# 24 weight tiles of the middle part are split beside the first feed-forward, by way of DRAM and GpSimd's queue

## The chip, the cores and the metric

The kernel runs on one core of a Trainium2 chip. The metric is the device time of one execution in microseconds (us). The engines are named as in the profile: PE is TensorE, PEld its weight load, DVE is VectorE, ACT is ScalarE, POOL is GpSimd and SP is SyncE, which only issues transfers here. "Line 154" or L154 is a line of the kernel before.

## What is computed

One layer of a decoder trunk for 1024 prompt tokens and 8 sample tokens, with 1024 columns:

```python
h = layer_norm(ALPHA * x + 0.5 * swiglu(x, ffn1_wg, ffn1_wu, ffn1_wd), ln1_g, ln1_b)
q_a, k_a, v_a, q_i, k_i, w_i, q_r, k_r, v_r, g_r = jnp.split(h @ w_in, _split_points(), axis=-1)
o_a = attend(q_a, k_a, v_a, q_i, k_i, w_i)      # indexer scores pick 256 keys per query, then softmax
o_r, s_new = retention(qr, kr, vr, s0)          # 4 heads of 128, in chunks
y_r = jax.nn.silu(g_r) * (group_norm(o_r) * ret_gn_g)
mix = jnp.concatenate([o_a, y_r], axis=-1) @ w_out
h = layer_norm(ALPHA * h + mix, ln2_g, ln2_b)
h = layer_norm(ALPHA * h + 0.5 * swiglu(h, ffn2_wg, ffn2_wu, ffn2_wd), ln3_g, ln3_b)
```

Each feed-forward has 2816 hidden columns. All data are float32.

## The kernel before

**Numbers.** Each float32 operand of a product is taken apart: ScalarE casts it to a shorter format (the high part, `wh_...` for a weight), another engine subtracts the cast from the original (the low part, `wl_...`), and TensorE does three products, high by high, high by low and low by high (`mm3`, lines 169 to 171). This is called splitting here. A weight tile is 1024x128, 512 KB, held as 128 partitions by 1024 values in one slot of SBUF; a split tile is three slots: raw (`wr_...`), high, low.

**Tokens** are processed in three chunks of 344 columns (`CW`); a product of a weight tile with a chunk is 24 matmuls into one PSUM bank.

**Stages.** The first feed-forward runs chunk 0 alone (0 to 274 us) and then chunks 1 and 2 together (`chunks12`, 274 to 699 us). The second pass takes pairs of hidden tiles: for each of 11 pairs a chain of seven products for the gate (`chain(p, 'G')`), the down products of the pair before (`down_pair`), and a chain of seven for the other factor (`chain(p, 'U')`). Its weights come through a `Stream`, which fetches raw tiles on SP, splits them on ScalarE and VectorE (`whole` for a down tile, `seven` for the two raw tiles of a chain), and takes its slots from a free list `g.fs` (22 slots in this pass); `keep` is how many slots it leaves free when it works ahead. `keep` is 1 throughout, since `chunks12` is called with `tight=0`. After it come the first layer norm and the first head's tiles (699 to 787), the indexer's scores (787 to 890), heads 1 to 3 of the retention beside the top-k search (890 to 1147), the attention's tiles and the attention (1147 to 1345), the output projection (1345 to 1465 for its first eight tiles), and the second feed-forward (in all to 2310).

**The top-k search** (`topk`) is a loop over 32 bits: the keys below a threshold are counted, on ScalarE (line 1034) for the longer key blocks and on VectorE (line 1037) for the shorter, then two small instructions on VectorE (lines 1044 and 1045) move the threshold of every query.

**The tiles of the middle part.** From the scores to the output projection, weight tiles go through one object, `wq = Weights(g, tiles)`. `tiles` is the list in order of use: 3 indexer tiles (`qi1` to `qi3`), `gr0`, then key, value, query and gate of heads 1 to 3, 12 tiles of the attention (`va`, `qa`, `ka`), 8 of the output projection (`wo0` to `wo7`) and more. `fetch` issues the load of the next raw tile on SP into the one raw slot; `split` (through `w_split`) casts it on ScalarE (line 152) and subtracts on the engine of `g.lo_eng`, GpSimd in this stretch (line 154), into one of two pairs of slots, and fetches the next; `get` hands over the split pair. `tile(...)` gets the running tile, does its three chunks, and calls `split` for the next after the first of them.

**Order.** The program's text is run by a planner, `Sched`: each stage is a generator, a `yield` of a number of units (about a microsecond each) puts it off by that much, and `s.tick(cost)` behind each group of matmuls moves the planned time on and lets the generators that are due emit their instructions. `s.drain(e)` ticks until a generator is at its end. When the program is built, each engine's instructions are then put in an order of their own, so that an engine's order need not be that of the text.

The change touches `Weights`, `trunk` (the call of `chunks12`, the hook `ready`, which runs ahead of each chain step, and the list of tiles).

Of the kernel before, what the change touches and what calls it, by code (L numbers as in the profile page):

```python
# [15 lines left out]
F32 = mybir.dt.float32  # L16
F32R = mybir.dt.float32r
# [5 lines left out]
OP = mybir.AluOpType  # L23
# [3 lines left out]
P = 128  # L27
# [15 lines left out]
class Sched:  # L43


    def __init__(self):
        self.t = 0.0
        self.gens = []
# [32 lines left out]
def setbanks(g, **kinds):  # L81
    g.banks = kinds
    g.bi = {k: 0 for k in kinds}
# [14 lines left out]
def A(g, slot, name, dt=F32, n=NTOK):  # L98

    return g.ap.tile([P, n], dt, tag=f"a{slot}", name=name, bufs=1)  # L100


def A8(g, slot, name, dt=F32):
    return A(g, slot, name, dt, 1024).rearrange("p (k f) -> p k f", k=8)
# [7 lines left out]
def X8(g, slot, name, dt=F32):  # L112
    return X(g, slot, name, dt).rearrange("p (k t) -> p k t", k=8)
# [24 lines left out]
def w_raw(g, src, name):  # L138
    s = g.raws[g.ri % len(g.raws)]
    g.ri += 1  # L140
    raw = A8(g, s, f"wr_{name}")
    g.nc.sync.dma_start(raw if len(src.shape) == 3 else raw.rearrange("p (k h) f -> p k h f", k=src.shape[1]), src)
    return raw, name


def w_split(g, raw):

    raw, name = raw
    a, b = g.pairs[g.pi % len(g.pairs)]
    g.pi += 1  # L150
    hi = A8(g, a, f"wh_{name}", F32R)
    g.nc.scalar.copy(hi, raw)
    lo = A8(g, b, f"wl_{name}", F32R)
    g.lo_eng[g.pi % len(g.lo_eng)].tensor_tensor(out=lo, in0=raw, in1=hi.bitcast(F32), op=OP.subtract)  # L154
    return hi, lo
# [6 lines left out]
def wcols(w, col):  # L162
    return w[:, col:col + 128].rearrange("(k p) f -> p k f", p=P)
# [44 lines left out]
class Stream:  # L208
# [12 lines left out]
    def fetch(self):  # L221
        g = self.g
        while self.todo and self.held < self.nraw and len(g.fs) > self.keep:
            key, src = self.todo.pop(0)
            sl = g.fs.get()
            self.held += 1
            t = A(g, sl, f"wr_{key[0]}_{key[1]}", F32, 1024)
            g.nc.sync.dma_start(t.rearrange("p (k f) -> p k f", k=src.shape[1]), src)
            self.raw[key] = (t, sl)
# [311 lines left out]
def halves_of(t):  # L541
    return t[:, 0:4, :], t[:, 4:8, :]
# [189 lines left out]
def load_x(g, xp, xs, x, B, z):  # L732
# [10 lines left out]
    for b in range(3):  # L743
        fetch(b)
    yield 0.1
    for b in range(9):
# [22 lines left out]
        if b + 3 < 9:  # L769
            fetch(b + 3)  # L770
# [1129 lines left out]
    nc.sync.dma_start(ascr[:, :, 1024:1032].rearrange("h p b -> p h b"), on)  # L1900


class Weights:


    def __init__(self, g, tiles, split=True):
        self.g, self.tiles = g, tiles
        self.raw, self.ready = [], None
        self.fetch()
        if split:  # L1910
            self.split()

    def fetch(self):
        while self.tiles and len(self.raw) < len(self.g.raws):
            self.raw.append(w_raw(self.g, *self.tiles.pop(0)))

    def split(self):
        if self.raw:
            self.ready = w_split(self.g, self.raw.pop(0))
            self.fetch()  # L1920

    def get(self):
# [28 lines left out]
def trunk(tc, i, o):  # L1951
    nc = tc.nc
    g = G()
    g.nc, g.tc, g.s = nc, tc, Sched()
    s = g.s
    S_ = Scope(tc)
    w_in = i['w_in'][0]
    w_out = i['w_out'][0]
    cp = S_("cp")
    dp = S_("dp", space=bass.MemoryType.DRAM)  # L1960
# [33 lines left out]
    B = {'B22': halves_of(X8(g, "hh2", "opB22", F32R))}  # L1994
    B['B11'], B['B21'] = [tuple(t[:, 4 * q:4 * q + 4, :] for t in x[1]) for q in range(2)]
    f1 = Ffn2(g, i['ffn1_wg'][0], i['ffn1_wu'][0], i['ffn1_wd'][0], z, "f1")
# [44 lines left out]
    def ready(p, i):  # L2041
        need = {2: 'T2', 3: 'T1', 4: 'T3', 6: 'T4'}.get(i)
        s.until(lambda: need is None or need in B)

    f1.chunk0(x[0], hook, parked)
    psum['out'] = True
    setbanks(g, ch=[0, 1, 2, 3], dn=[4, 5], aux=[6, 7])
    f1.chunks12(B, ready)


    S_.close("msF")
# [23 lines left out]
    own = [q for q in g.fs.ids if q in ok][:6]  # L2075
# [95 lines left out]
                rX['qr0'] = w_raw(g, wcols(w_in, colX['qr0']), 'qr0')  # L2171


    tiles = [(wcols(w_in, 1536 + 128 * ct), f"qi{ct}") for ct in (1, 2, 3)] + [(wcols(w_in, 3656), "gr0")]
    for hd in (1, 2, 3):
        tiles += [(wcols(w_in, c0 + 128 * hd), f"{n}{hd}") for c0, n in ((2632, "kr"), (3144, "vr"), (2120, "qr"), (3656, "gr"))]
    for ct in range(4):
        tiles += [(wcols(w_in, c0 + 128 * ct), f"{n}{ct}") for c0, n in ((1024, "va"), (0, "qa"), (512, "ka"))]
    rows = [(w_out[128 * k:128 * k + 128, :].rearrange("p (k f) -> p k f", k=8), f"wr{k}") for k in (2, 3)]
    halves = [[(w_out[r:r + 512, 256 * j:256 * j + 256].rearrange("(k p) (h f) -> p k h f", p=P, h=2), f"wh{r}_{j}") for j in range(4)] for r in (0, 512)]  # L2180
    tiles += [(wcols(w_out, 128 * oo), f"wo{oo}") for oo in range(8)] + rows + halves[1]
    g.raws, g.ri, g.pairs, g.pi = [0], 0, PAIRS[:2], 0
    g.lo_eng = [nc.gpsimd]
    g.mixlo = [nc.vector]
    wq = Weights(g, tiles)

    def tile(evac, name, pace=0.0):
        w = wq.get()
# [27 lines left out]
    t = A(g, 6, "gT0")  # L2216
# [8 lines left out]
    hi, lo = {}, {}  # L2225
# [18 lines left out]
    for hd in (1, 2, 3):  # L2244
# [8 lines left out]
        t = A(g, 6, f"gT{hd}")  # L2253
# [42 lines left out]
    for ct in (1, 2, 3):  # L2296
# [4 lines left out]
        q = (qx[:, 0:1024], qx[:, 1024:2048]) if ct % 2 else (A(g, 9, f"q0{ct}", F32R, 1024), A(g, 1, f"q1{ct}", F32R, 1024))  # L2301
# [73 lines left out]
    for oo in range(6):  # L2375
        w = wq.get()
# [3 lines left out]
    w = [wq.get()]  # L2380
# [18 lines left out]
    w = [wq.get()]  # L2399
# [21 lines left out]
    for j in range(4):  # L2421
        w = wq.get()
# [7 lines left out]
    wq = Weights(g, halves[0], False)  # L2430
# [3 lines left out]
    B = {}  # L2434
# [43 lines left out]
    own = {}  # L2478
# [87 lines left out]
```

## Time and profile before

| | |
|---|---|
| median of 3 runs | 2312.18 us (2311.66 to 2313.08) |
| the profiled execution | 2311.91 us |
| its span | 2310.1 us |
| TensorE busy | 2220.8 us, 96% of the span |
| VectorE busy | 1761.8 us, 76% |
| ScalarE busy | 1072.4 us, 46% |
| GpSimd busy | 323.4 us, 14% |
| mean granted clock of TensorE | 0.985 |

The durations come from one profiled execution. The time of an execution is its span and some 1.8 us around it. A busy share is a mean over stages with different limits, so the stages have to be looked at one by one: which engine is full in it, and which wait ends last. A wait shown for an instruction is its engine's idle time just before it, with the instruction that released it.

### The profile page before, as it was taken

Reading aid. Unit: us, or ns where it says so; the run is one execution under the profiler, and the core shown is the slowest. Engines: PE = TensorE matmul, PEld = TensorE weight load, DVE = VectorE, ACT = ScalarE, POOL = GpSimd, SP = SyncE. Lnnn points to the kernel's source line nnn. Section 1 sums busy time; section 2 is a strip of 40 time slices with the busy share of each in tenths; the row PEclk is TensorE's granted clock in tenths of the full one; section 3 lists DMA queues with packets and bytes.
Section 4 is the critical chain, followed back from the end, with each engine's and each line's share of the span. In section 5 each row is a group of like instructions: output and inputs, shape, how many; then the busy total and the mean of one; then the engine's idle time right before and its main releaser. Section 6 shows DMA issues by size and latency. Waiting matters only on the chain.

```text
span 2310.1 us, 36886 instructions
## 1 busy us (share of the span) xinstructions
PE 2220.8 (96%) x14155; PEld 2144.3 (93%) x14155; DVE 1761.8 (76%) x3745; ACT 1072.4 (46%) x1931; POOL 323.4 (14%) x342
## 2 busy tenths in 40 slices
PE   8999999999999999889899999889999999999996
PEld 8999999999999989778789989879799999999996
DVE  5655797887878578678966678988568789887866
ACT  5433343332334465878466665343435444333331
POOL 0000100000002303444122234313210000000002
PEclk9999999999999999999999999989999999999998
DMA  8544332222222211121332142336544332222211
GB/s 266 156 136 146 109 89 74 83 75 64 82 75 97 93 25 46 53 69 49 88 89 56 51 141 80 121 123 189 177 129 137 98 103 80 92 73 65 92 65 49
DMA packets 239182, 224.32 MB, mean 97 GB/s; under 512 B 13098, under 2 KB 219774, under 8 KB 238238
## 3 DMA queue, kind: packets, MB, share of 16 engines
q1 hardware_dynamic: 235166, 209.38, 30.0%
q0 software_dynamic: 3840, 12.59, 1.7%
q8 instruction: 111, 1.82, 0.3%
q14 instruction: 65, 0.53, 0.1%
HBM read 200.91 MB, written 22.59 MB: 97 GB/s over the span
## 4 chain that ended last, share of the span: by engine, by line
PE 78%; DVE 11%; ACT 6%; issue 3%; DMA 1%; POOL 0%; POOLq 0%; SPq 0%; DVEq 0%; ACTq 0%
PE pds_f L403 5%; PE pds_f L404 5%; PE pds_f L405 5%; PE pg_f L169 2%; PE pu_f L169 2%; PE pg_f L170 2%; PE pg_f L171 2%; PE pdp_f L403 2%; PE pu_f L171 2%; PE pu_f L170 2%; PE pdp_f L404 2%; PE pdp_f L405 2%; ACT ja L1034 2%; PE ps_f1U L169 2%; PE ps_f2G L170 2%
## 5 line engine op out<-in xcount | busy, mean ns | idle before, releaser
L407 DVE SCALAR_TENSOR_TENSOR z<-pds_f,z 128x344 f32<-128x344 f32 x320 | 164.6, 516 | 125.9 <-PE pds_f L405 124.7
L403 PE MATMUL pds_f<-gs_f,wh_f1ds 128*128 128x344 f32 x352 | 114.1, 325 | 0.1
L407 DVE SCALAR_TENSOR_TENSOR z<-pdp_f,z 128x344 f32<-128x344 f32 x160 | 80.0, 512 | 44.1 <-PE pdp_f L405 43.9
L403 PE MATMUL pds_f<-gs_f,wh_f2ds 128*128 128x344 f32 x352 | 113.4, 322 | 0.0
L405 PE MATMUL pds_f<-gs_f,wl_f1ds 128*128 128x344 f32 x352 | 113.2, 322 | 0.0
L404 PE MATMUL pds_f<-gs_f,wh_f1ds 128*128 128x344 f32 x352 | 113.1, 321 | 0.0
L405 PE MATMUL pds_f<-gs_f,wl_f2ds 128*128 128x344 f32 x352 | 112.4, 319 | 0.0
L404 PE MATMUL pds_f<-gs_f,wh_f2ds 128*128 128x344 f32 x352 | 112.4, 319 | 0.0
L1034 ACT ACTIVATE ja<-key,zt 128x1024 bf16<-128x1024 int16 (+5 forms) x90 | 93.7, 1041 | 34.6 <-DVE zt L1045 33.1
L723 POOL TENSOR_TENSOR yt<-yt,ln_b_rows 128x512 f32<-128x512 f32 (+1 forms) x9 | 12.0, 1352 | 570.3 <-ACT yt L722 570.3
L296 ACT CAST wS_f1G<-ws_f1G 128x512 fp32r<-128x512 f32 x44 | 25.0, 618 | 133.5 <-PE pds_f L404 68.1
L1508 ACT CAST p<-pT 128x512 fp32r<-128x512 f32 (+2 forms) x112 | 47.4, 433 | 54.1 <-PE pT L1504 41.9
L296 ACT CAST wS_f2G<-ws_f2G 128x512 fp32r<-128x512 f32 x44 | 25.7, 619 | 93.4 <-PE pds_f L405 80.7
L403 PEld LDWEIGHTS pds_f<-gs_f,wh_f1ds 128*128 128x128 f32 x352 | 66.8, 190 | 1.1 <-DVE z L407 0.3
L404 PEld LDWEIGHTS pds_f<-gs_f,wh_f1ds 128*128 128x128 f32 x352 | 66.7, 190 | 0.2
L405 PEld LDWEIGHTS pds_f<-gs_f,wl_f1ds 128*128 128x128 f32 x352 | 66.7, 189 | 0.0
L403 PEld LDWEIGHTS pds_f<-gs_f,wh_f2ds 128*128 128x128 f32 x352 | 66.2, 188 | 0.2 <-ACT gs_f L465 0.2
L404 PEld LDWEIGHTS pds_f<-gs_f,wh_f2ds 128*128 128x128 f32 x352 | 66.2, 188 | 0.0
L405 PEld LDWEIGHTS pds_f<-gs_f,wl_f2ds 128*128 128x128 f32 x352 | 66.1, 188 | 0.0
L612 POOL TENSOR_TENSOR lns_l<-z 128x344 f32<-128x344 f32 x3 | 2.8, 929 | 442.2 <-DVE z L407 428.0
L1509 DVE TENSOR_TENSOR p<-pT,p 128x512 fp32r<-128x512 f32 (+2 forms) x112 | 54.5, 497 | 8.7 <-ACT p L1508 7.5
L1470 ACT ACTIVATE z<-z,mn 128x896 f32<-128x896 f32 (+3 forms) x64 | 49.8, 778 | 20.0 <-DVE mn L1467 15.7
(815 smaller groups left out, 8651.0 us busy)
## 6 DMA issues: line engine op xcount, KB each, us to landing
wr_f1g<-in_ffn_wg_dram SPq DMA_DIRECT2D x22, 512.0 KB
wr_f1u<-in_ffn_wu_dram SPq DMA_DIRECT2D x22, 512.0 KB
wr_f1dp<-in_ffn_wd_dram SPq DMA_DIRECT2D x22, 512.0 KB
wr_f1G<-in_ffn_wg_dram SPq DMA_DIRECT2D x22, 512.0 KB
wr_f1U<-in_ffn_wu_dram SPq DMA_DIRECT2D x22, 512.0 KB
wr_f1ds<-in_ffn_wd_dram SPq DMA_DIRECT2D x22, 512.0 KB
wr_f2u<-in_ffn_wu_dram SPq DMA_DIRECT2D x22, 512.0 KB
wr_f2g<-in_ffn_wg_dram SPq DMA_DIRECT2D x22, 512.0 KB
```

The source lines that it names most:

```text
L169: g.nc.tensor.matmul(ps, w[0][:, k, :], x[0][:, k, :], start=first and i == 0, stop=False)
L170: g.nc.tensor.matmul(ps, w[0][:, k, :], x[1][:, k, :], start=False, stop=False)
L171: g.nc.tensor.matmul(ps, w[1][:, k, :], x[0][:, k, :], start=False, stop=last and i == n - 1)
L296: nc.scalar.copy(t[:, 0], src)
L403: g.nc.tensor.matmul(ps, wh[:, o, :], th, start=i == 0, stop=False)
L404: g.nc.tensor.matmul(ps, wh[:, o, :], tl, start=False, stop=False)
L405: g.nc.tensor.matmul(ps, wl[:, o, :], th, start=False, stop=i == len(grp) - 1)
L407: g.nc.vector.scalar_tensor_tensor(out=z, in0=ps, scalar=0.5 / ALPHA, in1=z, op0=OP.mult, op1=OP.add)
L1034: nc.scalar.activation(jk[:, 0:n], key[b], AF.Sign, bias=t[:, j:j + 1], scale=-1.0, accum_out=cnt[:, j:j + 1])
L1470: nc.scalar.activation(z[:, 0:n], z[:, 0:n], AF.Exp, bias=prev, scale=-1.0, accum_out=mn[:, 3:4])
L1508: nc.scalar.copy(ph[:, js, ts], ptv[:, js, ts])
L1509: nc.vector.tensor_tensor(out=pl[:, js, ts], in0=ptv[:, js, ts], in1=ph[:, js, ts].bitcast(F32), op=OP.subtract)
```

## The change

A generator `presplit` is started ahead of the first feed-forward. From the second pair of the two-chunk pass on (`g.plain` is false for p >= 1), once five slots of `g.fs` are free, it takes three of them. For each of 24 tiles (all of `tiles` but the attention's 12 and those after `wo7`) it fetches the raw tile with a transfer issued by GpSimd, casts it on ScalarE, subtracts on VectorE, fetches the next raw tile, and stores the high and the low part to a scratch in DRAM (`wscr`), again with transfers issued by GpSimd. The pauses are 2.0 and 13.5 units a tile. `chunks12` is called with `tight=11`, so that `keep` is 4 instead of 1 in all the gate chains, and `s.drain(ahead)` behind the pass lets the generator finish.

`Weights` is told in `made` which tiles lie split in the scratch. Such a tile is loaded as two parts of 512 KB by two transfers on SP, straight into its pair of slots, where a raw tile was cast and subtracted before; `fetch` leaves it alone. The order in which tiles are used is the same. The other 12 tiles of the attention, and those after `wo7`, are done as before.

```diff
+def presplit(g, tiles, wscr, made):
+    nc = g.nc
+    while g.plain or len(g.fs) < 5:
+        yield 0.5
+    own = [g.fs.get() for _ in range(3)]
+    def fetch(n):
+        raw = A8(g, own[0], f"pr_{tiles[n][1]}")
+        nc.gpsimd.dma_start(raw, tiles[n][0])
+        return raw
+    raw = fetch(0)
+    yield 8.0
+    for n, (src, name) in enumerate(tiles):
+        hi, lo = A8(g, own[1], f"ph_{name}", F32R), A8(g, own[2], f"pl_{name}", F32R)
+        nc.scalar.copy(hi, raw)
+        nc.vector.tensor_tensor(out=lo, in0=raw, in1=hi.bitcast(F32), op=OP.subtract)
+        yield 2.0
+        if n + 1 < len(tiles):
+            raw = fetch(n + 1)
+        for j, t in enumerate((hi, lo)):
+            nc.gpsimd.dma_start(wscr[n, j], t.rearrange("p k f -> p (k f)").bitcast(F32))
+        made[name] = (wscr[n, 0], wscr[n, 1])
+        yield 13.5
+    g.fs.put(*own)
 class Weights:
     def fetch(self):
-        while self.tiles and len(self.raw) < len(self.g.raws):
+        while self.tiles and self.tiles[0][1] not in self.made and len(self.raw) < len(self.g.raws):
             self.raw.append(w_raw(self.g, *self.tiles.pop(0)))
     def split(self):
-        if self.raw:
-            self.ready = w_split(self.g, self.raw.pop(0))
+        g = self.g
+        if not self.raw and self.tiles and self.tiles[0][1] in self.made:
+            name = self.tiles.pop(0)[1]
+            pair = g.pairs[g.pi % len(g.pairs)]
+            g.pi += 1
+            self.ready = tuple(A8(g, q, f"w{j}_{name}", F32R) for j, q in enumerate(pair))
+            for t, src in zip(self.ready, self.made[name]):
+                g.nc.sync.dma_start(t.rearrange("p k f -> p (k f)").bitcast(F32), src)
+            self.fetch()
+        elif self.raw:
+            self.ready = w_split(g, self.raw.pop(0))
             self.fetch()
     def ready(p, i):
         need = {2: 'T2', 3: 'T1', 4: 'T3', 6: 'T4'}.get(i)
         s.until(lambda: need is None or need in B)
+        g.plain = p < 1
+    made = {}
+    g.plain = True
+    ahead = s.add(presplit(g, list(tiles), dp.tile([len(tiles), 2, P, 1024], F32, name="wscr"), made))
-    f1.chunks12(B, ready)
+    f1.chunks12(B, ready, 11)
+    s.drain(ahead)
-    wq = Weights(g, tiles)
+    wq = Weights(g, tiles, True, made)
```

The list of the 24 tiles now stands ahead of the first feed-forward, and the attention's 12 tiles are put back into their place in it when `wq` is made.

## Rows read from the trace of the kernel before

**Rows 1.** The page, part 1: busy time, share and instructions by engine.

```profile
PE 2220.8 (96%) x14155; PEld 2144.3 (93%) x14155; DVE 1761.8 (76%) x3745; ACT 1072.4 (46%) x1931; POOL 323.4 (14%) x342
```

**Rows 2.** Busy us (instructions) by stage: PE, PEld, DVE, ACT, POOL; clock, DMA, GB/s.

```profile
0.00:274.00 274.00, 266.53 (x1678) 263.31 (x1679) 165.49 (x230) 113.99 (x168) 7.48 (x12) 0.99 0.55 165
...
274.00:699.00 425.00, 424.74 (x2696) 424.04 (x2695) 349.40 (x638) 157.99 (x277) 1.25 (x1) 1.00 0.27 79
...
787.00:890.00 103.00, 99.42 (x603) 93.03 (x602) 72.19 (x155) 60.38 (x113) 18.59 (x13) 0.98 0.13 35
...
890.00:1147.00 257.00, 228.43 (x1536) 212.02 (x1534) 210.06 (x555) 178.77 (x357) 103.40 (x115) 0.95 0.23 63
...
1345.00:1465.00 120.00, 110.61 (x755) 103.96 (x754) 100.19 (x371) 68.33 (x150) 42.28 (x48) 0.99 0.37 114
```

**Rows 3.** The chain of waits from 890 to 1147, its shares by line.

```profile
by line: ACT ja L1034 20.1%; issue 11.4%; DVE jv L1037 3.3%; DVE tief L1070 3.0%; DVE zt L1045 2.6%; DVE key L1054 2.2%; DVE zt L1044 2.0%; DVE tie L1069 2.0%; DVE tie L1068 1.7%; DVE tie L1075 1.7%; DVE o L1203 1.7%; DVE zt L982 1.5%; DVE 
```

**Rows 4.** Instructions of lines 154, 152: duration ns min/median/max, first and last start.

```profile
L154 POOL TENSOR_TENSOR wl_kr<-wr_kr,wh_kr x3: 2367/2382/2398, 873.8 to 1022.2; 128x1024 fp32r<-128x1024 f32 x3
...
L152 ACT CAST wh_kr<-wr_kr x4: 1045/1048/1051, 699.2 to 1020.2; 128x1024 fp32r<-128x1024 f32 x4
```

**Rows 5.** Timelines of DVE and POOL (start, us, engine, line), and line 1044's durations.

```profile
943.29 2.30 DVE L1044 TENSOR_TENSOR zt<-zt 128x6 f32<-128x6 f32 x1 [1.48 <-ACT ja L1034]
...
943.20 2.37 POOL L154 TENSOR_TENSOR wl_kr<-wr_kr,wh_kr 128x1024 fp32r<-128x1024 f32 x1
...
L1044 DVE TENSOR_TENSOR zt<-zt x32: 119/166/2359, 920.5 to 1107.1; 128x6 f32<-128x6 f32 x32
...
1065.79 2.40 DVE L627 SCALAR_TENSOR_TENSOR zt<-zt 128x8 f32<-128x8 f32 x1
```

**Rows 6.** Pieces of the chain of waits (start, us, what); TensorE's timeline.

```profile
929.53 0.95 ACT wh_gr L152
...
941.28 1.04 ACT wh_kr L152
...
1062.97 0.95 ACT wh_qr L152
...
961.29 0.40 PE L169 MATMUL pw_kr<-h1h,wh_kr 128*128 128x344 f32 x1
```

**Rows 7.** VectorE's timeline near 894 and 1416, and durations of lines 982 and 1680.

```profile
894.28 2.01 DVE L982 SCALAR_TENSOR_TENSOR zt<-rl,wsgn,zt 128x320 f32<-128x320 f32 x1 [1.94 <-ACT rl L977]
...
L982 DVE SCALAR_TENSOR_TENSOR zt<-rl,wsgn,zt x70: 543/677/2677, 807.5 to 899.0; 128x512 f32<-128x512 f32 x21, 128x384 f32<-128x384 f32 x21, 128x448 f32<-128x448 f32 x14, 128x320 f32<-128x320 f32 x14
...
1416.48 2.25 DVE L1680 SCALAR_TENSOR_TENSOR zt<-zt 128x1 f32<-128x1 f32 x1
...
L1680 DVE SCALAR_TENSOR_TENSOR zt<-zt x16: 146/160/2887, 1407.6 to 1492.9; 128x1 f32<-128x1 f32 x16
```

**Rows 8.** SP's timeline, busy time (as rows 2), and the gathers of tile s3kv.

```profile
913.52 0.37 SPq L142 DMA_DIRECT2D wr_gr<-in_w_in_dram  x1
...
914.50:917.00 2.50, 1.20 (x7) 1.21 (x8) 2.50 (x5) 0.00 (x0) 1.25 (x2) 1.00 0.79 210
...
L1788 POOL DMA_INDIRECT s3kv<-in_cache_k_dram,zt x16: 940/984/1869, 1541.5 to 1581.9; - x16
...
DMA to landing us min/median/max: 3.6/4.0/4.3
```

**Rows 9.** VectorE's groups from 312 to 690 (count | busy us, mean ns).

```profile
L274 DVE TENSOR_TENSOR wl_f1ds<-wr_f1ds,wh_f1ds 128x1024 fp32r<-128x1024 f32 x20 | 24.4, 1222 | 3.0 <-ACT wh_f1ds L273 2.9
```

**Rows 10.** Busy time in two stretches of the feed-forwards (as rows 2).

```profile
300.00:313.00 13.00, 13.00 (x85) 13.00 (x84) 12.74 (x26) 7.31 (x15) 0.00 (x0) 1.00 0.27 82
...
1844.00:1975.00 131.00, 131.00 (x841) 130.80 (x840) 115.95 (x229) 57.66 (x95) 0.00 (x0) 1.00 0.31 96
```

**Rows 11.** Timelines of ScalarE and TensorE at the end of the two-chunk pass.

```profile
688.18 1.06 ACT L152 CAST wh_ki<-wr_ki 128x1024 fp32r<-128x1024 f32 x1
...
698.83 0.32 PE L171 MATMUL ps_f1U<-opT,wA_f1U 128*128 128x344 f32 x1
```

More of the change, by code (lines that the diff above doesn't have):

```diff
@@ L1900, in s3_attend, with __init__ @@
     nc.sync.dma_start(ascr[:, :, 1024:1032].rearrange("h p b -> p h b"), on)
+def presplit(g, tiles, wscr, made):
[21 more added lines that the diff above has]
+    g.fs.put(*own)
 class Weights:
-    def __init__(self, g, tiles, split=True):
-        self.g, self.tiles = g, tiles
+    def __init__(self, g, tiles, split=True, made={}):
+        self.g, self.tiles, self.made = g, tiles, made
         self.raw, self.ready = [], None
@@ L2043, in ready @@
         s.until(lambda: need is None or need in B)
+        g.plain = p < 1
+    tiles = [(wcols(w_in, 1536 + 128 * ct), f"qi{ct}") for ct in (1, 2, 3)] + [(wcols(w_in, 3656), "gr0")]
+    for hd in (1, 2, 3):
+        tiles += [(wcols(w_in, c0 + 128 * hd), f"{n}{hd}") for c0, n in ((2632, "kr"), (3144, "vr"), (2120, "qr"), (3656, "gr"))]
+    tiles += [(wcols(w_out, 128 * oo), f"wo{oo}") for oo in range(8)]
+    made = {}
+    g.plain = True
+    ahead = s.add(presplit(g, list(tiles), dp.tile([len(tiles), 2, P, 1024], F32, name="wscr"), made))
     f1.chunk0(x[0], hook, parked)
@@ L2171, in trunk @@
                 rX['qr0'] = w_raw(g, wcols(w_in, colX['qr0']), 'qr0')
[L2174 to L2178, printed above, removed]
     rows = [(w_out[128 * k:128 * k + 128, :].rearrange("p (k f) -> p k f", k=8), f"wr{k}") for k in (2, 3)]
     halves = [[(w_out[r:r + 512, 256 * j:256 * j + 256].rearrange("(k p) (h f) -> p k h f", p=P, h=2), f"wh{r}_{j}") for j in range(4)] for r in (0, 512)]
-    tiles += [(wcols(w_out, 128 * oo), f"wo{oo}") for oo in range(8)] + rows + halves[1]
+    tiles = tiles[:16] + [t for ct in range(4) for t in ((wcols(w_in, 1024 + 128 * ct), f"va{ct}"), (wcols(w_in, 128 * ct), f"qa{ct}"), (wcols(w_in, 512 + 128 * ct), f"ka{ct}"))] + tiles[16:] + rows + halves[1]
     g.raws, g.ri, g.pairs, g.pi = [0], 0, PAIRS[:2], 0
```

## The prediction

> **What bounds the kernel now.** I read the page first: TensorE is busy for 96% of the span and GpSimd for 14% [rows 1], so the question is only where TensorE is not busy. The busy time by stage answers that [rows 2]. In the first feed-forward's two-chunk pass (274 to 699 us) TensorE has no gap: 2696 matmuls in 425 us, 6.34 per us, with VectorE at 349 of 425 us. In the score stage (787 to 890) it lacks 3.6 of 103 us, in the stage with heads 1 to 3 beside the top-k search (890 to 1147) 28.6 of 257 at a mean granted clock of 0.95, and beside the output projection (1345 to 1465) 9.4 of 120. The 24 tiles of the change are used in these last three stages. In the top-k stage the chain of waits does not run mainly through matmuls: the counts on ScalarE hold 20.1% of it, more than any other line [rows 3]. The loop is serial: ScalarE counts keys against a threshold, VectorE compares the counts and moves the threshold, then come the next counts. What stands in that loop lengthens the stage.
>
> **What is removed.** Each of the 24 tiles now costs a cast on ScalarE (1.05 us) and a subtraction on GpSimd (2.38 us) [rows 4], 25 us and 57 us in all. Neither engine is full there, so the sum is not these totals but what of them stands on the chain.
>
> First the subtractions. While GpSimd subtracts, VectorE can stand still: its threshold instruction on 128x6 values normally takes 0.166 us (the median) and took 2.30 us at 943.29, from 0.09 us after the start of a 2.37 us subtraction to its end [rows 5]. It happens four times in this stage to instructions of about 0.17 us, first here and last at 1065.79 (2.40 us) [rows 5]. All four fall on subtractions of this change's tiles and lie on or beside the chain; without these the instructions would give back 2.13 us (the first) to 2.23 (the last), 8.7 us together.
>
> Then the casts. Four of them are pieces of the chain in this stage, between two counts or ahead of the threshold, the first at 929.53, the last at 1062.97, 0.95 to 1.05 us each: 4.0 us [rows 6]. Together 12.7 us in the serial loop.
>
> Outside this loop three more VectorE instructions are held by subtractions: two score accumulations (2.01 us at 894.28, where 0.54 is the shortest, and the longest of them, 2.68 us where 0.68 is the median) and a 128x1 step of the sample's search at 1416.48 (2.25 us, median 0.16) [rows 7]: 1.5 + 2.0 + 2.1 = 5.6 us. I take nothing of it: in the score stage TensorE lacks only 3.6 of 103 us, so the matmuls take over the chain at once, and at the output projection the attention's own work runs beside the search. The bounds are therefore 4.0 (the casts alone: GpSimd's other work, 103 us busy in this stage less 12 subtractions of 2.4, moves up and holds VectorE instead) and 12.7 + 5.6 = 18.3 us. I take 12.7, since in the loop nothing else runs in parallel and TensorE has 28.6 us of gaps there to give.
>
> **What is added where the tiles are used.** Each tile is now two loads of 512 KB on SP in place of one. A 512 KB load issued at 913.52 moved data from 914.5 to 917 [rows 8], so about 3.4 us; a pair about 6 us. It can start when TensorE is done with the tile two before, as the cast can; the tile cast at 941.28 has its first matmul at 961.29 [rows 6], 20 us later. So the running tile's matmuls hide the loads and I cost them at nothing. Without that cover it would be some 6 us for each tile that finds SP late, for SP is in order and stores that wait for VectorE stand in front of the loads. The 12 tiles that stay (values, queries, keys of the attention) keep cast and subtraction.
>
> **What is added in the pass.** 24 casts (25 us of ScalarE) and 24 subtractions on VectorE at 1.22 us (29 us), 24 fetches and 48 stores issued by GpSimd, 38 MB. GpSimd has no work of its own there (1.25 us of 425), so nothing is moved behind these issues. The pass already does 20 whole-tile splits of exactly this shape between 312 and 690, with 1.22 us on VectorE each [rows 9], without a gap on TensorE. VectorE goes from 349 to 378 of 425 us, 89%. The second feed-forward ran like this: with six slots taken (eighteen left; nineteen here) and the same reserve of four, VectorE stood at 116 of 131 us, and TensorE did 841 matmuls in it, 6.42 per us, no slower [rows 10]. The traffic would be 79 + 89 = 168 GB/s, and the first pass of this feed-forward runs at 165 GB/s with TensorE busy. So the longer reserve and the three slots cost nothing by these rows. What can hurt is a subtraction in a stretch in which VectorE is full, as it is in the first chains of a pair (12.74 of 13 us [rows 10]). About a third of the 24 fall there, 8 x 1.22 = 9.8 us at most; four PSUM banks cover most of it. Between 0 and 9.8 I take 2, near the row of the second feed-forward.
>
> The change adds one wait that matters: ScalarE's cast waits for a fetch that GpSimd issued. Behind it in ScalarE's queue are the gate's silu and the casts of the products, behind these VectorE's products, and behind those TensorE's PSUM banks. No plain transfer issued by GpSimd is in this trace. The nearest are its gathers of 256 KB: 0.94 to 1.87 us to issue and 3.6 to 4.3 us to land [rows 8]. The fetch has 1024 pieces of 512 bytes where a gather has 128, so an issue may well be longer. After the cast there is a second wait of the same kind, for the store of the tile before.
>
> One rule of the Trainium skill speaks against the change. The trace first: beside a VectorE that is busy most of the time, the slowest gather took 1.87 us to issue and the quickest 0.94 [rows 8], so something can hold an issue for 0.9 us. "SBUF — State Buffer", section "SBUF: two separate sides", says that a transfer issued by GpSimd can stand until VectorE ends an instruction that uses both its ports, and the section "Summary: rules for kernel authors" says to issue from SP or ScalarE instead. The section "Who interferes with whom" does not count a subtraction of two tensors among these instructions, and two-tensor work is all that VectorE does in the pass, so by this page's own terms the rule would hardly bite here; no run shows it yet. If it bites, it is rival 5.
>
> **Sum.** The profiled execution took 2311.91 us (span 2310.1), 0.27 below the median of 2312.18. Against it: -12.7 + 2 = -10.7, so 2301.2; set against the median 2301.5 us.
>
> **The rivals.**
> 1. Late fetches: slower. The program's text is not the order on the engines: a cast whose line stands after the pass runs at 688.18, ten us before the pass's last matmuls end [rows 11]. So each engine's instructions were put in order beforehand, by when they were thought ready, and the splits will be pulled forward as far as their three slots allow. If a fetch then lands later than thought, ScalarE stands with the pass's work behind it. Each fetch waits for the subtraction before it, so lateness adds up: from 12.7 / 24 = 0.53 us a tile on, all is lost. With 0.6 us (a gather's 4.0 us landing against 3.4 from SP) plus 0.9 us (its slowest issue over its fastest), 1.5 x 24 = 36 us: 2312 - 12.7 + 36 = 2335.5. For it: an unseen kind of issue. Against it: nothing in the pass waits for a transfer now. Chance 0.18.
> 2. Another engine's work takes the place: GpSimd's rotations, decays and gathers move up and hold VectorE as the subtractions did, or TensorE's order in the stage binds; 4.0 us gained, 2 lost: 2310. Chance 0.17.
> 3. Everything on the chain is won: -18.3 and no loss in the pass: 2294. Chance 0.13.
> 4. Engine order follows the text at the pass's end. The splits are paced at 15.5 units, but a wait ends only at the next tick (1.89 in a chain, 0.94 in a down pass), so some 18; the pass has 426 units, the splits start near 40 (26.5 for the first pair, then seven steps, when by my count of the stream's slots five are first free) and only 21 of 24 fit. Three would then stand between the pass and its last part, two of them behind a fetch: 2.3 + 2 x (1 + 4.0 + 2.3) = 16.9 us less two PSUM groups of 1.9: +13, so 2312 + 13 + 2 - 12.7 = 2314. The row at 688.18 speaks against it. Chance 0.05.
> 5. Each issue in the pass is held as the slowest gather was, by 0.93 us, and all three of a tile stand in the loop of fetch, split and store: 24 x 3 x 0.93 = 67 us, so 2312 - 12.7 + 67 = 2366. That is the Trainium skill's rule of above. Against it: the pass has no VectorE instruction of one input alone. Chance 0.04.
>
> **How the numbers follow.** The forecast, 2301.5, has 0.43. A measurement of this kernel can tell about 0.2% (4.6 us) from no change. Faster: forecast and rival 3, 0.56. Same: rivals 2 and 4, 0.22. Slower: rivals 1 and 5, 0.22. The range goes from a little more than the whole chain won (2291) to a lateness of about 1 us a tile (2324).
>
> **What would show it.** Right: no subtraction of these tiles on GpSimd after 787, no threshold instruction of 2.3 us beside them, the stage from the first sort key to the last mask shorter by about 11 us, and 6.3 matmuls per us in the pass. Rival 1: the pass longer than 425 us and ScalarE's casts of the new tiles waiting for transfers. Rival 2: 2.3 us threshold instructions beside other GpSimd work. Rival 4: a hole of TensorE at the end of the pass. The prediction is wrong if the pass loses more than the top-k stage gains, which hangs on one number that the trace before does not hold: how long a 512 KB fetch issued by GpSimd takes.

## The result, and the profile after

The changed kernel is slower: median 2341.07 us (2338.76 to 2345.27) beside 2312.3 us for the kernel before on the same chip, ratio 1.0124, 95% interval 1.0112 to 1.0136. The profiled execution is the longest of the four, 2345.27 us with a span of 2343.4, 33.4 more than the span before. The prediction had the sign wrong, and its range (2291 to 2324) did not reach the time.

| profiled execution, us from its start | before | after | later by |
|---|---|---|---|
| last chain matmul of the two-chunk pass ends | 699.15 | 745.72 | 46.6 |
| first matmul of `ki` | 729.89 | 779.24 | 49.4 |
| first sort key | 885.48 | 929.40 | 43.9 |
| last mask of the search | 1156.59 | 1166.19 | 9.6 |
| first matmul of tile `va0` | 1108.18 | 1133.20 | 25.0 |
| first matmul of `wo0` | 1364.87 | 1397.52 | 32.7 |
| end | 2310.06 | 2343.42 | 33.4 |

The busy times of the whole execution hardly tell the two kernels apart; the page's first part answers to [rows 1]:

```profile
PE 2230.4 (95%) x14155; PEld 2152.1 (92%) x14155; DVE 1759.7 (75%) x3769; ACT 1072.4 (46%) x1931; POOL 315.2 (13%) x390
```

The table of times does: by the first matmul of `ki` the pass has lost 49 us, the stages up to the first matmul of `va0` win 24, and 8 of these are given back up to the first matmul of `wo0`. First the loss: the stage from 274 to 699 again (columns as in [rows 2]), then a stretch with down products and the stretch with chains behind it.

```profile
274.00:699.00 425.00, 391.94 (x2400) 385.89 (x2399) 331.25 (x594) 160.29 (x269) 49.04 (x73) 0.98 0.51 159
357.00:383.00 26.00, 23.32 (x147) 22.73 (x146) 15.32 (x28) 6.61 (x11) 5.94 (x9) 1.00 0.64 197
383.00:407.00 24.00, 23.39 (x148) 22.97 (x146) 24.00 (x46) 13.38 (x24) 0.00 (x0) 1.00 0.43 138
...
435.00:455.00 20.00, 16.85 (x107) 16.51 (x106) 20.00 (x38) 10.19 (x19) 0.00 (x0) 1.00 0.37 118
```

TensorE does 2400 matmuls in the 425 us in which it did 2696. There are two kinds of stretch: from 357 to 383 VectorE is busy for only 15.3 of 26 us, and from 383 to 407 and 435 to 455 it is full. What it did not do in the first it has to do in the second, and there TensorE waits for it (busy for 16.9 us from 435 to 455). The whole pass up to its last chain matmul, after and before:

```profile
274.00:745.70 471.70, 438.64 (x2696) 432.59 (x2695) 368.10 (x660) 180.53 (x302) 49.04 (x73) 0.98 0.49 151
```

```profile
274.00:699.10 425.10, 424.83 (x2696) 424.14 (x2695) 349.50 (x638) 157.99 (x277) 1.25 (x1) 1.00 0.27 79
```

Of the 46.6 us, 32.8 are idle time of TensorE. For the other 13.8 it is busy longer with as many matmuls, at a mean granted clock of 0.98 in place of 1.00; how much of this the clock alone takes is not separated here.

What it waits for stands in the timeline of one such stretch: ScalarE, GpSimd, VectorE and TensorE of the changed kernel. L1912 is the fetch of `presplit`, L1919 its cast, L1920 its subtraction, L1925 its stores; in brackets the idle time ahead and what ended it.

```profile
364.11 1.05 ACT L1919 CAST ph_kr<-pr_kr 128x1024 fp32r<-128x1024 f32 x1 [3.45 <-DMA pr_kr<-in_w_in_dram]
372.28 1.05 ACT L1919 CAST ph_vr<-pr_vr 128x1024 fp32r<-128x1024 f32 x1 [7.12 <-DMA pr_vr<-in_w_in_dram]
380.37 1.05 ACT L1919 CAST ph_qr<-pr_qr 128x1024 fp32r<-128x1024 f32 x1 [7.04 <-DVE z L407]
```

```profile
365.45 0.53 POOL L1925 DMA_DIRECT2D wscr<-ph_kr  x1 [5.14 <-ACT ph_kr L1919]
366.93 0.91 POOL L1912 DMA_DIRECT2D pr_vr<-in_w_in_dram  x1 [0.95 <-DVE pl_kr L1920]
367.83 0.54 POOL L1925 DMA_DIRECT2D wscr<-pl_kr  x1
```

```profile
365.41 1.23 DVE L1920 TENSOR_TENSOR pl_kr<-pr_kr,ph_kr 128x1024 fp32r<-128x1024 f32 x1 [1.68 <-DMA wscr<-pl_gr]
...
373.58 1.23 DVE L1920 TENSOR_TENSOR pl_vr<-pr_vr,ph_vr 128x1024 fp32r<-128x1024 f32 x1 [1.85 <-DMA wscr<-pl_kr]
```

```profile
367.11 0.43 PE L403 MATMUL pds_f<-gs_f,wh_f1ds 128*128 128x344 f32 x1 [1.26 <-DVE z L407]
375.29 0.42 PE L403 MATMUL pds_f<-gs_f,wh_f1ds 128*128 128x344 f32 x1 [1.43 <-DVE z L407]
```

The splits do not stand 15.5 units apart, as the text paces them. In the engines' own order they are packed three or four to a stretch of down products: of the 23 steps from one cast to the next, 16 are under 12 us, with a median of 8.19. One turn reads: subtraction done at 366.6, fetch issued at 366.93, low part's store issued right behind it at 367.83, cast at 372.28, when the fetch is in. The cast ends at 373.33, and the subtraction waits until 373.58 for the store of the low part of the tile before. Behind it in VectorE's order stand the accumulations of the down products (line 407), behind these TensorE. All over the pass:

```profile
ACT ph_wo L1919 <- DMA pr_wo<-in_w_out_dram: 54.2, 8, 9.7
ACT ph_gr L1919 <- DMA pr_gr<-in_w_in_dram: 20.0, 4, 8.4
ACT ph_vr L1919 <- DMA pr_vr<-in_w_in_dram: 19.3, 3, 8.9
```

```profile
PE pds_f L403 <- DVE z L407: 17.3, 12, 2.4
PE ps_f1G L169 <- DVE pc_f1U L469: 14.8, 6, 4.0
```

These are views of the waits, ScalarE's (three of its rows) and TensorE's: waiting instruction, releaser, us in total, times, longest. ScalarE stands 132 us in all, in 22 waits, ahead of the new casts for fetches, TensorE 17.3 us for accumulations in the down products and 14.8 us for VectorE at the chains' start.

The gain is of the kind that was forecast. Lines 1044 and 1045 in the changed kernel, and the search from its first sort key to its last mask, before and after:

```profile
L1044 DVE TENSOR_TENSOR zt<-zt x32: 152/166/783, 960.0 to 1120.4; 128x6 f32<-128x6 f32 x32
L1045 DVE SCALAR_TENSOR_TENSOR zt<-zt x32: 157/166/875, 960.2 to 1120.8; 128x6 f32<-128x6 f32 x32
```

```profile
885.50:1156.60 271.10, 241.54 (x1624) 223.76 (x1622) 223.98 (x589) 185.47 (x378) 103.40 (x115) 0.96 0.23 63
```

```profile
929.40:1166.20 236.80, 214.14 (x1478) 202.48 (x1477) 197.10 (x549) 166.72 (x338) 76.44 (x103) 0.96 0.27 85
```

No threshold instruction takes 2.3 us any more (783 and 875 ns at most, where [rows 5] show 2359), and the search is 34 us shorter. Not all of the 34 us is won: the search now holds 146 matmuls fewer, and the stretch from its last mask to the first matmul of `wo0` holds 145 more, before and after:

```profile
1156.59:1364.87 208.28, 202.53 (x1380) 189.45 (x1378) 140.52 (x431) 131.28 (x310) 55.88 (x72) 1.00 0.28 81
```

```profile
1166.19:1397.52 231.33, 225.63 (x1525) 209.77 (x1523) 152.00 (x471) 139.15 (x337) 56.06 (x72) 0.99 0.30 88
```

TensorE is busy for 97% of this stretch in both kernels, so the matmuls that left the search lengthen it: by 23 us. The pairs of loads that took the casts' place are issued early enough, as this line of SP's timeline shows (two loads, 0.80 us together). The first matmul of `kr1` comes at 938.99, and none of TensorE's waits from 730 to 1600 us ended with a transfer:

```profile
916.88 0.80 SPq L1953 DMA_DIRECT2D w_kr<-wscr  x2
```

### The profile page after: what moved, and what is told of

Its sections match the earlier page's. It is cut to its first block, busy times and chain, and to the rows that moved or that the text cites. A ratio compares the mean times of both kernels' runs of the same rounds, so it can differ in the third digit from the quotient of the medians.

```text
span 2343.4 us, 37108 instructions
## 1 busy us (share of the span) xinstructions
PE 2230.4 (95%) x14155; PEld 2152.1 (92%) x14155; DVE 1759.7 (75%) x3769; ACT 1072.4 (46%) x1931; POOL 315.2 (13%) x390
## 4 chain that ended last, share of the span: by engine, by line
PE 53%; DVE 12%; ACT 7%; DMA 5%; issue 3%; POOL 1%; POOLq 0%; DVEq 0%; ACTq 0%; SPq 0%
PE pds_f L403 3%; ACT ja L1034 3%; PE pds_f L404 3%; PE pds_f L405 3%; PE ps_f2U L170 2%; PE ps_f2G L170 2%; PE ps_f2G L169 2%; PE ps_f2U L171 2%; PE ps_f2G L171 2%; PE ps_f2U L169 2%; PE pg_f L169 1%; PE pg_f L170 1%; PE pu_f L169 1%; PE pg_f L171 1%; PE pdp_f L403 1%
## 5 line engine op out<-in xcount | busy, mean ns | idle before, releaser
L169 PE MATMUL pg_f<-xh,wh_f1g 128*128 128x344 f32 x176 | 57.0, 324 | 2.1 <-ACT xh L762 2.1
L169 PE MATMUL pg_f<-h2h,wh_f2g 128*128 128x344 f32 x176 | 58.5, 332 | 0.0
```

Source lines behind the costliest of these rows:

```text
L169: g.nc.tensor.matmul(ps, w[0][:, k, :], x[0][:, k, :], start=first and i == 0, stop=False)
```

## The experiments

Theory L, formed after the result: a split's cast and subtraction wait for transfers that arrive late, and the pass's own work stands behind them. The rivals are the plain work of the splits, the slots they take, and the stores. All times are medians; the kernel before was measured beside each group, and its median lies between 2312.3 and 2314.8 us.

**The cost alone.** The tiles are split and stored, and done again later as before.

```diff
-    wq = Weights(g, tiles, True, made)
+    wq = Weights(g, tiles, True, {})
```

> The splits in the first feed-forward are made and stored, but nothing uses them: all 24 tiles are cast and subtracted later as in the kernel before. So this is the price of the pass by itself. Theory L (late transfers: ScalarE and VectorE stand at a split until its fetch and the store of the tile before have landed, with the pass's own work queued behind them): the pass ends some 47 us later, as it does in the changed kernel (745.7 for 699.2), and nothing gives it back: 2312 + 47 = 2359, between 2352 and 2366. The forecast's price of the pass was 2 us: 2314.

Measured: 2367.04 beside 2314.77 us (1.0229, 1.0212 to 1.0246). The last chain matmul ends at 748.51. The kernel loses 52 us, 1 more than the end of L's range and 50 more than forecast.

**The gain alone.** In `presplit`, only the first tile:

```diff
     for n, (src, name) in enumerate(tiles):
+        if n:
+            made[name] = (wscr[0, 0], wscr[0, 1])
+            continue
...
-        if n + 1 < len(tiles):
-            raw = fetch(n + 1)
```

> Only the first tile is split and stored in the feed-forward; all 24 are then loaded from its place in the scratch, so 23 of the tiles hold wrong weights. This is the gain of the use by itself. In the changed kernel the delay falls from 49 us ahead of the scores to 33 at the output projection, so theory L expects 16 us of gain: 2296, between 2293 and 2300. The forecast's 12.7 us would give 2299.5. If what was gained beside the top-k search is given back later whatever stands ahead, 2305 to 2312.

Measured: 2296.85 us (0.9929, 0.9912 to 0.9945), 17.9 less than before. Cost and gain nearly add up: 52.3 - 17.9 = 34.4, for 28.8 between the medians and 33.4 between the spans of the changed kernel. Loading each tile as a pair costs nothing that shows. This kernel keeps the larger reserve, and takes the three slots for its one tile: its first matmul of `ki` comes at 734.74, 4.9 us later than before, and from there to the end it wins 20.1 us. The 17.9 are thus a gain of 20 less a small part of the price.

**The slots alone.** The body of `presplit` between taking and giving back the slots becomes 24 pauses.

```diff
+    for _ in tiles:
+        yield 15.5
```

> The three slots are taken for as long as in the changed kernel and the longer reserve stays, but nothing is fetched, split, stored or used. Theory L: no price, 2312, between 2309 and 2315. Rival R (the three slots and the reserve of four starve the pass's own stream of weights): most of the 47 us, 2340 or more.

Measured: 2317.85 us (1.0014, 1.0004 to 1.0023), 3.1 more than before. That is above L's range and far below R's: taking three slots and a longer reserve is not quite free, but it is no cause of 50 us.

**The work alone**: one fetch, one pair of stores, 24 casts and subtractions.

```diff
-        if n + 1 < len(tiles):
-            raw = fetch(n + 1)
         for j, t in enumerate((hi, lo)):
-            nc.gpsimd.dma_start(wscr[n, j], ...)
-        made[name] = (wscr[n, 0], wscr[n, 1])
+            if n == 0:
+                nc.gpsimd.dma_start(wscr[n, j], ...)
+        made[name] = (wscr[0, 0], wscr[0, 1])
```

> One tile is fetched once and stored once, but all 24 casts and 24 subtractions are made, from that one raw tile, and all 24 tiles are loaded later from the one place in the scratch, so 23 tiles hold wrong weights. It has the work of the splits on ScalarE and VectorE without any wait for a transfer. Theory L: the work alone costs 0 to 6 us, so with 16 us of gain 2296 to 2302. Rival W (54 us more work on two engines that were already the second bound, above all 29 us on VectorE): 20 us or more of the 47, so 2316 or more.

Measured: 2300.06 us (0.9939, 0.9923 to 0.9956), 3.2 above the gain alone. The pass, by its busy times and by the first casts on ScalarE's timeline:

```profile
274.00:700.00 426.00, 424.31 (x2687) 422.83 (x2686) 369.98 (x659) 180.68 (x301) 3.46 (x4) 1.00 0.26 82
```

```profile
323.19 1.05 ACT L1919 CAST ph_gr<-pr_qi 128x1024 fp32r<-128x1024 f32 x1 [1.29 <-DVE pl_qi L1920]
325.53 1.05 ACT L1919 CAST ph_kr<-pr_qi 128x1024 fp32r<-128x1024 f32 x1 [1.29 <-DVE pl_gr L1920]
327.87 1.05 ACT L1919 CAST ph_vr<-pr_qi 128x1024 fp32r<-128x1024 f32 x1 [0.94 <-DVE pl_kr L1920]
```

The splits are packed closer still, 2.34 us apart, and TensorE is busy for 424.3 of 426 us all the same. So neither the work nor its packing by itself is the cause: rival W falls, and the 41 us up to 2341 come with the transfers (43.5 if each kernel is counted from the kernel before of its group).

**Fetch or store.** First the edit without refetching (the two lines `if n + 1 < ...` taken out), then the one with a single pair of stores (the other edit of the work alone).

> One fetch for all: every split is made from the first raw tile, with both its stores, and every tile is loaded from its own place, so 23 tiles hold wrong weights. The cast waits for no fetch any more; the waits for the stores stay. Theory F (the fetch is what a split waits for: ScalarE stood 132 us ahead of the new casts for fetches, VectorE 27 us for stores): most of the 41 us between the work alone (2300) and the changed kernel (2341) goes: 2300 to 2312. Rival S (the stores and their traffic hold the loop): 2325 to 2341.

> Every raw tile is fetched and split, but only the first is stored, and all 24 are loaded from its place, so 23 tiles hold wrong weights. The waits for stores and a store's transfer beside each fetch are gone; the wait for the fetch stays. Theory F: most of the 41 us stays: 2325 to 2341. Rival S: 2300 to 2312. If fetch and store share the price, because the low part's store is issued right behind the next fetch and moves its data at the same time, both of these runs lie between.

| fetches | stores | median us | last chain matmul ends | consecutive casts under 12 us apart, median |
|---|---|---|---|---|
| 1 | 1 pair | 2300.06 | 702.28 | 2.34 |
| 1 | 24 pairs | 2307.09 | 707.57 | 5.33 |
| 24 | 1 pair | 2321.82 | 725.00 | 7.30 |
| 24 | 24 pairs (changed kernel) | 2341.07 | 745.72 | 8.19 |

The kernel with fetches alone keeps 22 us of the 41, the one with stores alone 7, and 12 come only with both: a fetch beside a store arrives later (5.37 us from issue to cast in the changed kernel, 4.65 without the stores, medians of 24 casts, 22 of which waited for their fetch). The kernel with stores alone lies where theory F had it; the one with fetches alone is 3 us below F's range, so that the fetch leads but the two share the price. Counted from the kernel before of each group the shares are 22, 7 and 15 of 43.5 us.

**The issuing engine.** `nc.gpsimd.dma_start` becomes `nc.sync.dma_start` in the fetch and the stores.

> The changed kernel with its 24 fetches and 48 stores issued by SP in place of GpSimd; nothing is left out. A fetch issued by GpSimd with little else moving landed after 4.76 us (the first one of the kernel with the work alone); a load of the same size issued by SP took 3.4 us before. Theory F with a price for the issuing engine: 24 x 1.4 = 33 us less, 2308. Rival Q (the wait is the loop of fetch, split and store, whoever issues; and on SP the stream's own loads stand behind an issue that waits for a split): 2335 or more.

Measured: 2315.78 beside 2314.82 us (1.0007, 0.9998 to 1.0017): 25 us of the 41 are gone with the issuing engine alone, 8 fewer than theory F's 33. From issue to cast a fetch now takes 4.65 us in place of 5.37, and the issue itself 0.38 in place of 0.91. Rival Q falls by the time, but the loop that it speaks of is still there: ScalarE stands 105 us for fetches ahead of 22 of the new casts, where it stood 132.

**A second raw slot.** Fetches are issued one split ahead, from four slots.

```diff
-    while g.plain or len(g.fs) < 5:
+    while g.plain or len(g.fs) < 6:
...
-        raw = A8(g, own[0], f"pr_{tiles[n][1]}")
+        raw = A8(g, own[3 * (n % 2)], f"pr_{tiles[n][1]}")
...
-    raw = fetch(0)
+    raws = [fetch(0), fetch(1)]
...
-        if n + 1 < len(tiles):
-            raw = fetch(n + 1)
+        if n + 2 < len(tiles):
+            raws.append(fetch(n + 2))
```

> A second raw slot: the fetch of a tile is issued when the split two before it is done, so that it has a whole split more to land; four slots are taken in place of three, and the wait for slots asks for six. Nothing is left out. Theory F: the fetch is hidden and what is left is the stores' part, 2300 to 2315. Rival P (the splits are only put closer together in each engine's order, and wait as before): 2325 to 2341.

Measured: 2442.2 us, 127 more than before, which neither theory expected. GpSimd's timeline gives the reason:

```profile
686.28 1.10 POOL L1912 DMA_DIRECT2D pr_qi<-in_w_in_dram  x1 [409.41 <-DVE wl_f1ds L274]
```

Six slots are not free until the pass is all but over (its chains end at 700.33, 1.2 us later than before), so the 24 splits come behind it, with casts from 691 to 890. TensorE is busy for only 60 us from 700 to 898. The run says nothing on prefetching, but it prices splits without cover: TensorE's first matmul of `kr0` comes at 898, 168 us later than before. The wait for six goes back to five:

> Two raw slots again, each fetch issued one split ahead, but four slots are taken as soon as five are free, so that the splits do start in the pass (with the wait for six they started only at its end). GpSimd issues; nothing is left out. Theory F with interaction (of the 41 us of transfers, 22 are the fetch, 7 the stores, 12 both together, since the low part's store moves beside the next fetch): with the fetch a split ahead only the stores' 7 us stay: 2307, between 2303 and 2314. Rival P (the loop only runs faster and then waits for the same transfers): 2325 or more.

> As the run with two raw slots taken at five, with all transfers issued by SP. Theory F: issue by SP took 25 us from the price (2315.8), the second raw slot takes the rest of the fetch: 2301 to 2307, the kernel with the work alone being 2300. Rival Q (with a fetch a split ahead the issuing engine no longer matters, but SP's order holds the stream's loads): as the run with GpSimd or slower, 2307 to 2320.

Measured: 2321.73 us with GpSimd issuing, beside 2313.67 (1.0037, 1.0023 to 1.0051), and 2306.29 with SP (0.9969, 0.9958 to 0.9981). With GpSimd that is neither theory's range, 8 above F's and 3 below P's; with SP it is F's, and rival Q falls. A fetch that is a split ahead takes 19 us of the 41 away with GpSimd and 9 of the 16 that were left with SP. VectorE's timeline of the run with GpSimd shows what the loop hangs on now (the subtraction is line 1921 there):

```profile
361.48 1.22 DVE L1921 TENSOR_TENSOR pl_kr<-pr_kr,ph_kr 128x1024 fp32r<-128x1024 f32 x1 [1.55 <-DMA wscr<-pl_gr]
369.56 1.23 DVE L1921 TENSOR_TENSOR pl_vr<-pr_vr,ph_vr 128x1024 fp32r<-128x1024 f32 x1 [1.79 <-DMA wscr<-pl_kr]
```

The turn is 8.1 us long as before, but ended by the store of the low part, which moves beside the next fetch.

**Slots taken anew** for each tile, the raw one at the fetch, two at the split eight units later, all given back behind the stores:

```diff
+        while len(g.fs) < 2:
+            yield 0.5
+        q = g.fs.get()
...
+        yield 8.0
+        while len(g.fs) < 3:
+            yield 0.5
+        a, b = g.fs.get(), g.fs.get()
...
+        g.fs.put(q, a, b)
+        yield 4.0
...
```

> Each tile takes its slots anew from the free list, the raw one at its fetch, the other two eight units later at its split, and gives all three back, where the changed kernel holds three slots for all tiles. So no tile waits for the stores of the tile before, and a fetch is not tied to the split before it. GpSimd issues; nothing is left out. Theory F: no split waits for a transfer, 2300 to 2306. Rival R (slots are short: the pass's own stream waits for the slots that the stores hold): 2315 or more.

Measured: 2320.98 us (1.0034, 1.0023 to 1.0046). The casts wait only 22 us for fetches now, and 5 of the 23 steps between casts are under 12 us, but the pass's own stream now waits, for its own loads and for the slots that the stores hold, as rival R had it:

```profile
DVE ws_f1U L291 <- DMA wr_f1U<-in_ffn_wu_dram: 7.5, 3, 3.1
...
ACT wA_f1G L296 <- DMA wscr<-pl_gr: 3.2, 1, 3.2
```

**Two complete sets.** The low part is written over the raw tile, so that four slots hold two tiles in flight.

```diff
-        raw = A8(g, own[0], f"pr_{tiles[n][1]}")
+        raw = A8(g, own[n % 2], f"pr_{tiles[n][1]}", F32R)
...
+        if n + 1 < len(tiles):
+            raws.append(fetch(n + 1))
+        raw = raws.pop(0)
+        hi = A8(g, own[2 + n % 2], f"ph_{name}", F32R)
+        nc.scalar.copy(hi, raw.bitcast(F32))
+        nc.vector.tensor_tensor(out=raw, in0=raw.bitcast(F32), in1=hi.bitcast(F32), op=OP.subtract)
...
```

> Two complete sets of two slots: the low part is written over the raw tile, so that a tile takes two slots and four slots hold two tiles. A fetch waits for the stores of the tile two before, and a split for no store of the tile just before. GpSimd issues; nothing is left out. If the remaining 21 us are the loop through the single pair of slots: 2300 to 2308. If they are GpSimd's transfers as such: 2315 or more, as with two raw slots.

> The same two sets with all transfers issued by SP; nothing is left out. If the single pair of slots was the rest: 2300 to 2304, level with the work alone (2300.1) and no better than with GpSimd by more than 4 us. If the issuing engine was: 2300 to 2304 too, but 12 us or more below the run with two sets and GpSimd. If SP's order holds the stream's loads: 2306 or more.

Measured: 2327.22 us with GpSimd beside 2313.2 (1.0049, 1.0032 to 1.0066), 2301.65 with SP (0.9947, 0.9931 to 0.9964). The pass with GpSimd, then with SP:

```profile
274.00:700.00 426.00, 406.42 (x2545) 401.80 (x2544) 351.92 (x630) 168.81 (x284) 49.39 (x73) 1.00 0.49 162
```

```profile
274.00:700.00 426.00, 422.43 (x2664) 419.09 (x2663) 365.39 (x654) 179.00 (x300) 1.24 (x1) 1.00 0.50 164
```

The same bytes per second (162 and 164 GB/s), the same work, but 119 matmuls fewer with GpSimd. It is not the amount of traffic that costs. Two sets alone do not do it: with GpSimd the kernel is still 14 us slower than before, no better than with two raw slots, and SP is 25.6 below it. So by both expectations the issuing engine decides here, and not the single pair of slots. With SP and two sets the kernel stands within 3 us of the work alone (each counted from the kernel before of its group) and 11.6 us below the kernel before: it is faster than both kernels of this study. Yet the wait that theory F names is not gone in either, as one row of ScalarE's waits from each shows, with GpSimd and with SP:

```profile
ACT ph_wo L1922 <- DMA pr_wo<-in_w_out_dram: 31.9, 8, 13.1
```

```profile
ACT ph_wo L1922 <- DMA pr_wo<-in_w_out_dram: 27.4, 6, 11.3
```

In all ScalarE stands 91 us for fetches ahead of 22 new casts with GpSimd and 68 us ahead of 20 with SP, since a fetch now waits for the store of the tile two before (with GpSimd the one at 346.61 for 2.64 us). Beside the work alone that goes with a price of 29 us in one kernel and of 3 in the other, so the total of such waits is no price.

**Fewer tiles**: `presplit` gets `tiles[:16]`, without those of the output projection.

> The changed kernel with 16 of its 24 tiles split ahead, those of the indexer and the heads; the eight of the output projection are cast and subtracted as before. Nothing is left out of the result. In the trace of the changed kernel the output projection gains nothing (32.7 us late at its start, 32.1 at its end). If the price goes by the tile: 2341 less a third of the 44 us that the pass costs, 2341 - 15 = 2326, between 2320 and 2331. If it does not (the first pairs pay most of it): 2333 or more.

Measured: 2331.24 us (1.0075, 1.0058 to 1.0092), 5 above the expectation and at the very end of its range. The price of the pass does go by the tile: 34.3 us later at the first matmul of `ki`, 2.1 us for each of 16, as 49.4 is for each of 24. The median is 10 us below the changed kernel's and not 15. The profiled spans are 13.3 apart: from the first matmul of `ki` on, 14.2 us are won in place of 16.0, and the changed kernel's profiled execution is 4 us above its median.

## Why the prediction was wrong

**The pass, costed at 2 us, costs 49 to 52.** This is the step that failed: the sum put the new wait, ScalarE's cast for a fetch that GpSimd issued, at nothing and left it to rival 1. The row behind the 2 us, 20 whole-tile splits by the pass's own stream at 1.05 and 1.22 us without a gap [rows 9], was taken for the same thing because the two instructions have the same shape. The work alone shows that this half was right: 3 us. With the transfers come the other 41. What differs is what stands ahead of them. The stream fetches through SP, up to four raw tiles ahead, and takes other slots for each tile; `presplit` fetches into the slot that the split before has just left, so every split has its own transfer in its loop. The text puts 15.5 units between them, and I leaned on text for the pace while arguing, under rivals 1 and 4, that the text is not the order.

**Rival 1 was what happened.** Its mechanism (splits pulled forward, ScalarE standing with the pass's work behind it, lateness adding up) is that of the trace, and the point from which it decides, 0.53 us a tile, was passed nearly fourfold: 49.4 / 24 = 2.06 us, where I had priced 1.5 from the gathers' rows [rows 8] (36 us, 2335.5). The missing 0.5 us fits the stores, whose wait I named and did not price: the two-by-two table gives the stores and their meeting with the fetch 19 of 41 us. Little of this is the wait that I named, since a subtraction that a store held stood only 0.24 us (the median of 16) behind the end of its cast; from issue to cast a fetch takes 0.72 us longer beside a store. What I held against it, that nothing in the pass waits for a transfer, is an observation on transfers issued well ahead, and no evidence on one that is not. That the price came out within 6 us of rival 1's 2335.5 is in part luck, for the gathers' rows were a stand-in for a fetch that no row held. Its chance of 0.18 was too low, and the range ended at a lateness of 1 us.

**Rival 5 did not happen, but its advice was sound.** Every fetch took 0.91 us to issue (0.909 to 1.101) with VectorE busy or not, so no issue was held; that agrees with what the Trainium skill, "SBUF — State Buffer", "Who interferes with whom", says of subtractions of two tensors. Yet moving the issues to SP, as its "Summary: rules for kernel authors" advises for transfers under VectorE's work, gave 25 us, and between 15 and 26 in all three forms tried (one raw slot, two, two sets). By the issue times the rule's reason does not act here. What differs is the landing: a fetch with nothing beside it landed 4.8 us after its issue by GpSimd and a store 3.5 (the work alone), where SP's load took 3.4 [rows 8].

**The gain was right in kind and short in size.** Forecast 12.7, measured 17.9 by itself (20.1 from the first matmul of `ki` on) and 16 net in the changed kernel; rival 3 had 18.3. Two of the four held instructions that I counted in the search's loop are not threshold instructions but steps of an inverse root for the retention (line 626 at 986.86 and line 627 at 1065.79); both lie on the chain of waits all the same, with 2.31 and 2.41 us. The threshold instructions held for over 1.6 us are gone, also the two of 2.34 and 1.65 us (line 1045 at 945.69 and 1025.38 in the timeline before) that stood beside another GpSimd product (line 1145), which I had left in. Of rival 2, that other GpSimd work would take the subtractions' place, little is left: one threshold instruction of 783 ns beside that product and one of 875 ns beside a rotation (line 1116). The stage shrank by 34 us and not 11, but some 23 of these are matmuls that now stand behind the search, and 16 were left at the output projection. There I had taken 0, and that held: 32.7 us late at its start, 33.6 at the first matmul of the second feed-forward. In the score stage, where I had taken 0 too, 5.5 were won.

**Smaller points.** The reserve and the slots, costed at nothing, cost 3 us. Rival 4 (tiles left over behind the pass) did not occur in the changed kernel: its last cast is at 664, 82 us ahead of the pass's end. The kernel that waits for six slots has all 24 left and loses 127 us, 5.3 a tile, so three would cost some 16 by this estimate, near the 13 that I gave them.

**What stays open.** Each variant gets an engine order of its own, so the 15 to 26 us between the issuing engines hold a change of order beside the later arrival, and no run separates the two: from issue to cast only 0.72 us a tile (17 us for 24) are measured. Open too is why two sets cost 29 us beside the work alone with GpSimd and 3 with SP, though the casts wait for fetches in both.

## What to carry to other kernels

An instruction pair that is free in one place may be free there because its data came early: before costing a copy of it elsewhere at nothing, look at how many transfers ahead its source is issued, and through how many slots. A loop of fetch, work and store through one set of slots hands part of its round trip to everything queued behind it: here 41 us for 24 turns, most of them of 8 us. Two sets and the issuing engine whose fetches land sooner turned 29 us of loss into 12 of gain, with the same work and bytes; two sets alone left a loss of 14. And where a planner reorders the engines, pauses in the text need not hide anything: here 16 of 23 steps of 15.5 units became steps of 8 us.

## What the runs showed of the hardware

A 512 KB fetch of 512-byte pieces issued by GpSimd took 0.91 us to issue (1.10 for the first). It landed after 4.8 us with no store beside it (the work alone) and after 5.3 us beside stores (the median of 24 in the kernel with the cost alone). From issue to cast it was 5.4 us in the changed kernel, and with SP 4.65, of which the issue took 0.38. Stores of 4 KB pieces took 0.54 us to issue on GpSimd; the two of the work alone landed after 3.5 us. The fit in the Trainium skill, "DMA: Bandwidth & Descriptors", "Anatomy of one DMA — SWDGE (gpsimd) path", takes 2.0 us and adds the bytes divided by 436e3 a us, so an estimate for either would be 3.2 us: near the store, and 1.6 us short for the fetch. In the pass the granted clock fell too. TensorE was busy for 16.9 us from 435 to 455 and for 25.5 from 455 to 482, both at 1.00, and from 482 to 505 the clock was 0.85; it was 0.91 to 0.94 in four more stretches, a mix of the levels 1.2 and 2.4 GHz, where it was 1.00 throughout before [rows 2].
